# Contraction order, PSUM banks and the last gate tile of a one-core hybrid decoder layer

## The chip, the cores and the metric

The kernel runs on one core of one Trainium2 chip. A core has five engines with an instruction queue each: TensorE (PE), VectorE (DVE), ScalarE (ACT), GpSimd (POOL) and SyncE (SP); PEld in the profile is TensorE's loading of weights. The metric is the device time of one execution in microseconds; less is better.

## What is computed

One decoder layer on 512 tokens and 1024 features, all in float32. The core of the reference:

```python
x = x + 0.5 * swiglu(rmsnorm(x, ffn1_norm[i]), ffn1_wgu[i], ffn1_wdown[i])
h = rmsnorm(x, mix_norm[i])
z = h @ w_in[i]
zq, zk, zv, zc, zg = [z[..., offs[j]:offs[j + 1]] for j in range(len(SPLIT_SIZES))]
...
a = sliding_window_attention(q, k, v, sinks[i]) @ attn_proj[i]
...
u = causal_depthwise_conv(u, dw_w[i], dw_b[i])
c = jax.nn.silu(layernorm(u, conv_ln_g[i], conv_ln_b[i])) @ conv_proj[i]
ga, gb = jnp.split(zg, 2, axis=-1)
merged = jax.nn.sigmoid(ga) * a + jax.nn.sigmoid(gb) * c
x = x + merged @ w_out[i]
x = x + 0.5 * swiglu(rmsnorm(x, ffn2_norm[i]), ffn2_wgu[i], ffn2_wdown[i])
e = rmsnorm(p[i] @ ple_proj[i], ple_norm[i])
gate = jax.nn.sigmoid(rmsnorm(x, ple_gate_norm[i]) @ ple_gate_w[i])
x = x + gate * e
```

The attention has 16 query heads and 2 key/value heads of 64, a window of 128 tokens and a sink per head. `p` has 256 features.

## The kernel before

**Layout.** The activations lie with features on the 128 partitions and the 512 tokens in the free dimension: the residual is eight tiles `x[o]` of 128x512. A weight piece is 128x1024. PSUM is used as eight banks of 128x512.

**Products.** Each float32 product is made of three (`mm3`, L753): every operand is split into a rounded high half and the rest, and high by high, high by low and low by high are summed. For activations `split` makes the high half on ACT and the low half by a DVE instruction: the tiles `..._h` and `..._l`. For weights `piece` (L728) loads `raw_`, makes `whi_` on ACT and `wlo_` by a subtraction on DVE, or on DVE or POOL, whichever comes free first, for the keys in `FLEX`. For the keys in `SUMMED` (L404), the mixer's `wzc` and `wzg`, `residue` (L742) does it: ACT writes the negated rounded copy into `wlo_`, and a DMA on POOL's queue adds `raw_` to it. There are four buffers each of `raw`, `hi` and `lo` (L681).

**Stages.** FFN1, the mixer, FFN2 and the final gate follow one another on PE. The FFNs make most products in units of seven half-size products (`unit`, L972, products 1, 2, 6, 5, 7, 3, 4). `down` (L1122) adds the down products to the residual, half a tile at a time: the last unit for the first half of the outputs completes tiles 0, 1 (with product 7) and 4, 5 (product 4), that for the second half tiles 2, 3 and then 6, 7. When a tile is complete `next_norm` (L1167) splits it for the next stage (`mix_h`, `pg_h`) and adds its square to a running sum (`..._ss_acc`). The norm's factor per token is applied behind the products.

The mixer begins with keys and values: `keys_values` (L1277) calls `token_major` (L1253), whose contraction runs over the eight tiles `mix_h0` to `mix_h7` in order; two banks hold two token blocks each, and the whole contraction runs first for token blocks 0 and 1, then for 2 and 3. Queries (`wq`) go through the same function with a bank for each token block. The projections `ca`, `cb` (convolution and its gate), `ga`, `gb` (the two merge gates) are `proj` (L1180): 24 matmuls of 128x512 into a bank. `scores` (L1323), for one of two head groups `g` and one of four token blocks `t`, transposes the queries (`qTp`), then makes two groups of 12 matmuls (`jp` = 0, 1), each into two banks `sc`, each followed by the copies of ACT and the masked copies of DVE into the tiles `s` that empty them. `softmax` (L1362) makes exponentials on ACT, the denominators `den` with a reciprocal on DVE, and the normalization of `s` on POOL and ACT; `values` (L1382) transposes these (`pT`) and multiplies (`o`). The convolution is a long series of DVE instructions (`cz`) for five channel tiles, of ACT and POOL instructions for three.

`embedding` (L1485) makes the eight tiles `es` of the projected `p` during FFN2: ACT copies them out and squares them (`ple_sq`), POOL adds the squares, PE sums over partitions (`ple_cs`), and DVE multiplies each tile by its gain and by the norm's factor.

At the end, the loop from L1546 makes for each `o` the gate's product `pg` from all `pg_h` (`proj`, 24 matmuls), multiplies by the norm's factor (`wide_rstd`, whose products are `pg_mb`), takes the sigmoid on ACT, multiplies by `es`, adds to `x[o]` and stores. For the last tile these steps, but not the product, go by halves of 256 tokens.

**What sets the order.** `record` (L684) writes the program down; a planner (`plan`, L671) then orders it in the function `simulate` (L412), with costs and due times for each instruction and a list of PE groups (`nc.group`), and only then are the instructions of each engine written out (`hybrid_layer`, L1577). A group of matmuls is placed as a whole. An edit in one place can so move instructions on each engine elsewhere. `nc.flex` leaves to the planner whether DVE or POOL gets an instruction. All instructions are issued from one line, L1606, so that in the profile a group is told by its tiles.

Of the kernel before, what the change touches and what calls it, by code (L numbers as in the profile page):

```python
# [12 lines left out]
AF = mybir.ActivationFunctionType  # L13
# [3 lines left out]
P = 128  # L17
S = 512
# [665 lines left out]
def record():  # L684
    nc = Program()

    def ps_tile(name):
        return nc.tile(name, [P, S], F32, "ps")
# [70 lines left out]
    def part(w, s):  # L759
        return w[0][:, s], w[1][:, s]  # L760
# [85 lines left out]
    class SumSq:  # L846
# [3 lines left out]
        def add(self, v, on_act=False, accs=1):  # L850
# [11 lines left out]
                eng.tensor_tensor(acc, acc, to, op=ALU.add)  # L862
            self.n += 1

        def in_psum(self, v, last):

            n = self.n = self.n + 1
            to = ftile(f"{self.name}_sq{n}")
            nc.scalar.activation(to, v, AF.Square)
            if n == 1:  # L870
                self.run, self.one = ps_tile(f"{self.name}_acc"), to
            else:
                a = self.one if n == 2 else self.run
# [293 lines left out]
    def next_norm(tag, gain):  # L1167
        h, ss = [None] * KD, SumSq(f"{tag}_ss")

        def after(o):  # L1170
            h[o] = split(f"{tag}_h{o}", x[o], gain[:, o : o + 1])
            ss.in_psum(x[o], KD)

        return h, ss, after

# [4 lines left out]
    def proj(tag, key, i, h, nk=KD):  # L1180

        w = piece(key, i)
        ps = ps_tile(tag)
        with nc.group(tag):
            for k in range(nk):
                mm3(ps, part(w, slice(k * P, (k + 1) * P)), h[k], k == 0, k == nk - 1)
        return ps

    us, ys, pas = [None] * KD, [None] * KD, [None] * KD

# [59 lines left out]
        nc.gpsimd.tensor_tensor(z3[:, :, 0:16], z3[:, :, 0:16], cos, op=ALU.mult)  # L1250
        nc.gpsimd.tensor_tensor(z3[:, :, 0:16], z3[:, :, 0:16], w, op=ALU.add)

    def token_major(tag, key, i0, n_pieces, kper, n):  # L1253

        per = S // n
        banks = [ps_tile(f"{tag}b{b}") for b in range(NT // per)]
        pss = [banks[t % len(banks)][:, (t // len(banks)) * n :][:, 0:n] for t in range(NT)]
        ws = [piece(key, i0 + i) for i in range(n_pieces)]
        with nc.group(tag):
            for t0 in range(0, NT, len(banks)):  # L1260
                for i in range(n_pieces):
                    for kk in range(kper):
                        k = i * kper + kk
                        wk = part(ws[i], slice(kk * n, (kk + 1) * n))
                        for t in range(t0, t0 + len(banks)):
                            xk = part(h2[k], slice(t * P, (t + 1) * P))
                            mm3(pss[t], xk, wk, k == 0, k == KD - 1)
        return pss


# [4 lines left out]
    vf = nc.tile("vf", [P, NT, NKV, HD], F32, "a")  # L1275

    def keys_values():  # L1277
        pss = token_major("kv", "wkv", 0, 2, 4, 2 * P)
        norm2()
        k3s = []  # L1280
        for t in range(NT):
            z = nc.tile(f"zk{t}", [P, NKV, HD], F32, "a")
            p4 = pss[t].rearrange("p (b d) -> p b d", d=HD)
            r = r2k[:, t : t + 1]
            nc.scalar.activation(z, p4[:, 0:2], AF.Copy, scale=r)
            nc.scalar.activation(vf[:, t], p4[:, 2:4], AF.Copy, scale=r)
# [36 lines left out]
    def scores(g, t):  # L1323
# [12 lines left out]
        s = [nc.tile(f"s{g}_{t}_{i}", [P, 2, 2, W], F32, "a") for i in range(2)]  # L1336
        m = small(f"m{g}_{t}", 8)
        keys = slice(t0 * W, (t + 1) * W)
        for jp in range(2):
            banks = [ps_tile(f"sc{g}_{t}_{jp}{hh}") for hh in range(2)]  # L1340
            bs = [b.rearrange("p (j c k) -> p j c k", j=2, c=2) for b in banks]
            with nc.group(f"sc{g}_{t}_{jp}"):
                for j in range(2):
                    cols = slice((2 * jp + j) * P, (2 * jp + j + 1) * P)
                    for n, (a, b) in enumerate(((1, 0), (0, 0), (0, 1))):
                        for hh in range(2):
                            r = slice(hh * HD, (hh + 1) * HD)
                            nc.tensor.matmul(bs[hh][:, j, 0:nb], qT[a][r, cols], kT[b][r, keys], start=n == 0, stop=n == 2)
            for hh in range(2):
                sj = s[jp][:, :, hh]  # L1350
                if t == 0:
                    nc.vector.tensor_tensor(sj, bs[hh][:, :, 0], later, op=ALU.add)
                else:
                    nc.scalar.copy(sj, bs[hh][:, :, 1])
                    nc.vector.copy_predicated(sj, later.bitcast(I32), bs[hh][:, :, 0])
            mj = m[:, 4 * jp : 4 * jp + 4].rearrange("p (j h) -> p j h", h=2)
            nc.vector.tensor_reduce(mj, s[jp], axis=AX.X, op=ALU.max, negate=True)
# [127 lines left out]
    def embedding(i):  # L1485
# [7 lines left out]
        for j in range(4):  # L1493
# [4 lines left out]
                    c = (j * KP + k) * P  # L1498
                    mm3(ps, part(w, slice(c, c + P)), pin[k], k == 0, k == KP - 1)
            e = ftile(f"es{n}")  # L1500
            nc.scalar.copy(e, ps)
            es.append(e)
            sse.add(ps, on_act=True)
        if len(es) == KD:
            rbe = spread("ple", mean_rstd("ple", sse.accs, D))
            for o in range(KD):
                nc.vector.scalar_tensor_tensor(
                    es[o], es[o], g_ple[:, o : o + 1], rbe, op0=ALU.mult, op1=ALU.mult
                )

    steps = {
        "e": embedding,
# [31 lines left out]


    rb4 = None  # L1546
    for o in range(KD):
        ps = proj(f"pg{o}", "wgate", o, h4)
        if o == 0:
            rb4 = wide_rstd("pg", ss4.accs[0])  # L1550
        gt = ftile(f"gt{o}")
        n = S // 2 if o == KD - 1 else S
        for c in range(0, S, n):
            v = slice(c, c + n)
            nc.vector.tensor_tensor(gt[:, v], ps[:, v], rb4[:, v], op=ALU.mult)
            nc.scalar.activation(gt[:, v], gt[:, v], AF.Sigmoid)
            nc.vector.tensor_tensor(gt[:, v], gt[:, v], es[o][:, v], op=ALU.mult)
            nc.vector.tensor_tensor(x[o][:, v], x[o][:, v], gt[:, v], op=ALU.add)
# [160 lines left out]
```

## Time and profile before

| | before |
|---|---|
| runs, median (lowest to highest) | 1156.57 us (1155.35 to 1157.95) |
| profiled execution | 1154.82 us |
| its span in the trace | 1153.1 us |
| granted clock, mean | 0.999 |
| read from memory, written | 141.40 MB, 2.10 MB |

The profiled execution's span runs from its first instruction to its last; 1.7 us lie around it. In the rows of a timeline the first number is the start in us, the second the duration; x and a count joins rows of a kind, and the square bracket gives the idle time of the engine ahead of the row and what released it. PE's matmuls overlap: a row's duration is longer than the distance to the next start. The keys and values begin at 344.45 us, the embedding's sum `ple_cs` is made at 1014.36 us, and the gate begins at 1100.76 us.

### The profile page before, as it was taken

What the parts mean: (1) busy time and instruction counts of PE and PEld (TensorE: products, weight loads), DVE (VectorE), ACT (ScalarE), POOL (GpSimd) and SP (SyncE); (2) the same over time, 40 slices, a digit from 0 to 9 for tenths busy, and PEclk for the clock granted to TensorE, in tenths of its full rate; (3) what the DMA queues carried; (4) which work ended last, traced back from release to release, by engine and by line L of the source; (5) the groups of instructions that cost most, each with busy time, mean ns of one, the idle gap of its engine ahead of it and who ended that gap; (6) DMA issues with size and microseconds to landing.
All of it is one profiled execution on the core that took longest, in us unless ns stands there. A gap on an engine that the chain in (4) does not pass through costs nothing.

```text
span 1153.1 us, 19900 instructions
## 1 busy us (share of the span) xinstructions
PE 1140.8 (99%) x7484; PEld 1043.0 (90%) x7484; DVE 967.0 (84%) x1643; ACT 713.5 (62%) x1267; POOL 398.7 (35%) x481
## 2 busy tenths in 40 slices
PE   9999999999999999999999999999999999999998
PEld 7899999999998888878888888888999999999976
DVE  7799978889896799988997865579988788589995
ACT  7655446655366799999984753355654566673541
POOL 1632114222023886875786100035211132251000
PEclk9999999999999999999999999999999999999999
DMA  7456666566547472665654532335666655665421
GB/s 242 125 158 147 183 148 164 142 161 159 134 123 199 109 169 70 147 155 133 150 148 128 128 110 92 99 84 165 147 172 143 158 153 132 151 165 138 128 73 73
DMA packets 52511, 161.55 MB, mean 140 GB/s; under 512 B 6336, under 2 KB 13120, under 8 KB 52416
## 3 DMA queue, kind: packets, MB, share of 16 engines
q1 hardware_dynamic: 39312, 114.12, 30.1%
q0 software_dynamic: 12960, 46.14, 23.5%
q8 instruction: 58, 0.95, 0.3%
q14 instruction: 37, 0.30, 0.1%
q10 hardware_dynamic: 144, 0.03, 0.0%
HBM read 141.40 MB, written 2.10 MB: 124 GB/s over the span
## 4 chain that ended last, share of the span: by engine, by line
PE 94%; ACT 3%; DVE 2%; issue 0%; POOL 0%; DMA 0%; DVEq 0%; POOLq 0%; ACTq 0%
PE wgu_b L1606 17%; PE wgu_a L1606 12%; PE wd_b L1606 10%; PE wd_a L1606 8%; PE f_g L1606 5%; PE f_u L1606 5%; PE gb L1606 4%; PE ap L1606 4%; PE wo L1606 4%; PE cp L1606 4%; PE pg L1606 3%; PE cb L1606 3%; PE ga L1606 3%; PE ca L1606 3%; PE q0b L1606 2%; PE q1b L1606 2%
## 5 line engine op out<-in xcount | busy, mean ns | idle before, releaser
L1606 DVE TENSOR_TENSOR wlo_wgu<-raw_wgu,whi_wgu 128x1024 fp32r<-128x1024 f32 (+1 forms) x141 | 139.8, 1005 | 37.9 <-ACT whi_wgu L1606 37.6
L1606 ACT ACTIVATE whi_wgu<-raw_wgu 128x1024 fp32r<-128x1024 f32 (+1 forms) x141 | 115.4, 838 | 81.1 <-PE wgu_b L1606 32.7
L1606 ACT ACTIVATE whi_wd<-raw_wd 128x1024 fp32r<-128x1024 f32 (+1 forms) x60 | 59.3, 989 | 93.2 <-PE wd_b L1606 62.8
L1606 PE MATMUL wgu_b<-f_t_h,wlo_wgu 128*128 128x256 f32 x408 | 115.5, 283 | 0.0
L1606 PE MATMUL wgu_b<-f_t_l,whi_wgu 128*128 128x256 f32 x408 | 115.5, 283 | 0.0
L1606 PE MATMUL wgu_b<-f_t_h,whi_wgu 128*128 128x256 f32 x408 | 115.5, 283 | 0.0
L1606 POOL TENSOR_TENSOR y<-y,ct 128x511 f32<-128x511 f32 (+27 forms) x90 | 108.4, 1247 | 10.5 <-DVE wlo_wap L1606 5.0
L1606 DVE SCALAR_TENSOR_TENSOR cz<-u,dww,cz 128x510 f32<-128x510 f32 (+28 forms) x145 | 106.5, 735 | 3.3
L1606 POOL DMA_DIRECT2D raw_wgu<-in_wgu x34 | 29.8, 876 | 175.2 <-DMA raw_wgu<-in_wgu 53.3
L1606 PEld LDWEIGHTS wgu_b<-f_t_h,whi_wgu 128*128 128x128 f32 x408 | 78.3, 192 | 0.0
L1606 PEld LDWEIGHTS wgu_b<-f_t_h,wlo_wgu 128*128 128x128 f32 x408 | 78.3, 192 | 0.0
L1606 PEld LDWEIGHTS wgu_b<-f_t_l,whi_wgu 128*128 128x128 f32 x408 | 78.3, 192 | 0.0
L1606 PE MATMUL wgu_a<-f_nl,whi_wgu 128*128 128x256 f32 x272 | 77.0, 283 | 0.0
L1606 PE MATMUL wgu_a<-f_nh,wlo_wgu 128*128 128x256 f32 x272 | 77.0, 283 | 0.0
L1606 PE MATMUL wgu_a<-f_nh,whi_wgu 128*128 128x256 f32 x272 | 77.0, 283 | 0.0
L1606 DVE TENSOR_TENSOR wlo_wd<-raw_wd,whi_wd 128x1024 fp32r<-128x1024 f32 (+1 forms) x60 | 68.5, 1141 | 8.6 <-ACT whi_wd L1606 8.2
L1606 PE MATMUL wd_a<-f_f_h,wlo_wd 128*128 128x256 f32 x264 | 74.7, 283 | 0.0
L1606 PE MATMUL wd_a<-f_f_h,whi_wd 128*128 128x256 f32 x264 | 74.7, 283 | 0.0
L1606 PE MATMUL wd_a<-f_f_l,whi_wd 128*128 128x256 f32 x264 | 74.7, 283 | 0.0
L1606 PE MATMUL wd_b<-f_f_h,wlo_wd 128*128 128x256 f32 x264 | 74.7, 283 | 0.0
L1606 PE MATMUL wd_b<-f_f_h,whi_wd 128*128 128x256 f32 x264 | 74.7, 283 | 0.0
L1606 PE MATMUL wd_b<-f_f_l,whi_wd 128*128 128x256 f32 x264 | 74.7, 283 | 0.0
(505 smaller groups left out, 4041.2 us busy)
## 6 DMA issues: line engine op xcount, KB each, us to landing
raw_wgu<-in_wgu SPq DMA_DIRECT2D x76, 512.0 KB, 4.3
raw_wgu<-in_wgu POOLq DMA_DIRECT2D x34, 512.0 KB, 5.5
raw_wd<-in_wd SPq DMA_DIRECT2D x32, 512.0 KB, 4.5
raw_wd<-in_wd POOLq DMA_DIRECT2D x16, 512.0 KB, 5.5
raw_wzc<-in_wzc SPq DMA_DIRECT2D x16, 512.0 KB, 4.1
wlo_wzc<-raw_wzc POOLq DMA_DIRECT2D x16, 512.0 KB, 5.3
raw_wzg<-in_wzg SPq DMA_DIRECT2D x16, 512.0 KB, 4.6
wlo_wzg<-raw_wzg POOLq DMA_DIRECT2D x16, 512.0 KB, 5.8
```

Of the source, the lines that this page charges most:

```text
L1606: made[op] = getattr(engines[op.eng], op.what)(*a, **k)
```

## The change

1. `SUMMED` gets `wgate=0`: all eight gate weight pieces have their low half made by ACT and an accumulating DMA of POOL's queue.
2. `DONE = 0, 1, 4, 5, 2, 3, 6, 7`, the order in which `down` completes the residual tiles, becomes the order of the contraction for keys and values and for the first two gate tiles. These two (`proj2`) are each made as two groups of four feature tiles, which the planner may place apart.
3. `token_major` gives every token block a bank of its own, and runs through the contraction once: each feature tile is used for all four token blocks in turn. The queries had four banks already.
4. With `WHOLE` the 24 score matmuls of a block form one group into four banks, and the copies out of the banks come behind it.
5. `embedding` folds the gain into ACT's copy; what is left is a product with the norm's factor on DVE or POOL (the planner gives all eight to POOL).
6. The last gate tile is made by two groups of 24 matmuls of 128x256, each for 256 tokens and in a bank of its own (`halves`), each followed by its own steps. The other tiles go through `halves` in one piece.

`in_sbuf` isn't used, `INSB` being empty. In matmuls nothing is added but the 24 of part 6.

```diff
-SUMMED = dict(wzc=0, wzg=0)
+SUMMED = dict(wzc=0, wzg=0, wgate=0)
+WHOLE = True
+DONE = 0, 1, 4, 5, 2, 3, 6, 7
...
+    def halves(tag, key, i, h, cuts):
+        w = piece(key, i)
+        out = []
+        for c in range(cuts):
+            v = slice(c * S // cuts, (c + 1) * S // cuts)
+            out.append(ps_tile(f"{tag}_{c}"))
+            with nc.group(f"{tag}_{c}"):
+                for k in range(KD):
+                    mm3(out[c][:, v], part(w, slice(k * P, (k + 1) * P)), part(h[k], v), k == 0, k == KD - 1)
+        return out
+
+    def proj2(tag, key, os, h):
+        out = {}
+        for n in range(2):
+            for o in os:
+                if n == 0:
+                    out[o] = piece(key, o), ps_tile(f"{tag}{o}")
+                w, ps = out[o]
+                with nc.group(f"{tag}{o}_{n}"):
+                    for k in DONE[4 * n : 4 * n + 4]:
+                        mm3(ps, part(w, slice(k * P, (k + 1) * P)), h[k], k == DONE[0], k == DONE[-1])
+        return {o: ps for o, (w, ps) in out.items()}
...
-    def token_major(tag, key, i0, n_pieces, kper, n):
-        per = S // n
-        banks = [ps_tile(f"{tag}b{b}") for b in range(NT // per)]
-        pss = [banks[t % len(banks)][:, (t // len(banks)) * n :][:, 0:n] for t in range(NT)]
+    def token_major(tag, key, i0, n_pieces, kper, n, ks=range(KD)):
+        pss = [ps_tile(f"{tag}b{t}")[:, 0:n] for t in range(NT)]
         ws = [piece(key, i0 + i) for i in range(n_pieces)]
         with nc.group(tag):
-            for t0 in range(0, NT, len(banks)):
-                for i in range(n_pieces):
-                    for kk in range(kper):
-                        k = i * kper + kk
-                        wk = part(ws[i], slice(kk * n, (kk + 1) * n))
-                        for t in range(t0, t0 + len(banks)):
-                            xk = part(h2[k], slice(t * P, (t + 1) * P))
-                            mm3(pss[t], xk, wk, k == 0, k == KD - 1)
+            for k in ks:
+                i, kk = divmod(k, kper)
+                wk = part(ws[i], slice(kk * n, (kk + 1) * n))
+                for t in range(NT):
+                    xk = part(h2[k], slice(t * P, (t + 1) * P))
+                    mm3(pss[t], xk, wk, k == ks[0], k == ks[-1])
...
-        pss = token_major("kv", "wkv", 0, 2, 4, 2 * P)
+        pss = token_major("kv", "wkv", 0, 2, 4, 2 * P, DONE)
...
+        bss = []
         for jp in range(2):
...
-            with nc.group(f"sc{g}_{t}_{jp}"):
+            if not (WHOLE and jp):
+                cm = nc.group(f"sc{g}_{t}_{jp}")
+                cm.__enter__()
...
+            if not WHOLE or jp:
+                cm.__exit__(None, None, None)
+        for jp, bs in enumerate(bss):
...
-            nc.scalar.copy(e, ps)
+            nc.scalar.activation(e, ps, AF.Copy, scale=g_ple[:, n : n + 1])
...
-                nc.vector.scalar_tensor_tensor(
-                    es[o], es[o], g_ple[:, o : o + 1], rbe, op0=ALU.mult, op1=ALU.mult
-                )
+                nc.flex.tensor_tensor(es[o], es[o], rbe, op=ALU.mult)
...
+    gates = proj2("pg", "wgate", (0, 1), h4)
     for o in range(KD):
-        ps = proj(f"pg{o}", "wgate", o, h4)
+        ps = [gates[o]] if o in gates else halves(f"pg{o}", "wgate", o, h4, 2 if o == KD - 1 else 1)
```

On PE, in the keys' and values' contraction, the passage from the third to the fourth feature tile of before (`mix_h2`, `mix_h3`, the first pass over the banks `kvb0` and `kvb1`):

```order
L1606 MATMUL kvb1_4384<-whi_wkv0_4297,mix_h2_l_4346 128x256
L1606 MATMUL kvb1_4384<-whi_wkv0_4297,mix_h2_h_4331 128x256
L1606 MATMUL kvb1_4384<-wlo_wkv0_4336,mix_h2_h_4331 128x256
L1606 MATMUL kvb0_4379<-whi_wkv0_4297,mix_h3_l_4403 128x256
L1606 MATMUL kvb0_4379<-whi_wkv0_4297,mix_h3_h_4387 128x256
L1606 MATMUL kvb0_4379<-wlo_wkv0_4336,mix_h3_h_4387 128x256
```

and the passage from the second to the third in the changed kernel:

```order
L1646 MATMUL kvb3_4398<-whi_wkv0_4297,mix_h1_l_4232 128x256
L1646 MATMUL kvb3_4398<-whi_wkv0_4297,mix_h1_h_4155 128x256
L1646 MATMUL kvb3_4398<-wlo_wkv0_4337,mix_h1_h_4155 128x256
L1646 MATMUL kvb0_4379<-whi_wkv1_4341,mix_h4_l_4239 128x256
L1646 MATMUL kvb0_4379<-whi_wkv1_4341,mix_h4_h_4191 128x256
L1646 MATMUL kvb0_4379<-wlo_wkv1_4393,mix_h4_h_4191 128x256
```

The third tile used is now tile 4, from the second weight piece, after 24 matmuls for tiles 0 and 1; tile 3 comes sixth.

On PE, in the second head group's scores, the end of token block 1 and what follows (`sc1_1_10` is a bank of group 1, block 1, second pair of heads), before:

```order
L1606 MATMUL sc1_1_10_6243<-kTh_4818,qT1_1_h_6173 128x256
L1606 MATMUL sc1_1_11_6247<-kTh_4818,qT1_1_h_6173 128x256
L1606 MATMUL sc1_1_10_6243<-kTl_4835,qT1_1_h_6173 128x256
L1606 MATMUL sc1_1_11_6247<-kTl_4835,qT1_1_h_6173 128x256
L1606 MATMUL sc1_2_00_6271<-kTh_4818,qT1_2_l_6192 128x256
L1606 MATMUL sc1_2_01_6275<-kTh_4818,qT1_2_l_6192 128x256
```

and in the changed kernel:

```order
L1646 MATMUL sc1_1_10_6247<-kTh_4814,qT1_1_h_6173 128x256
L1646 MATMUL sc1_1_11_6250<-kTh_4814,qT1_1_h_6173 128x256
L1646 MATMUL sc1_1_10_6247<-kTl_4822,qT1_1_h_6173 128x256
L1646 MATMUL sc1_1_11_6250<-kTl_4822,qT1_1_h_6173 128x256
L1646 MATMUL gb7_6270<-mix_h0_h_4124,wlo_wzg15_6083 128x512
L1646 MATMUL gb7_6270<-mix_h0_h_4124,whi_wzg15_6094 128x512
```

The scores of block 2 are moved behind the 24 matmuls of the projection `gb7`, which followed them before. In the same manner the block `sc0_3` is moved behind the projections `cb4` and `cb5`, which followed it, and `ca6` now stands between `sc1_0` and `sc1_3`. On DVE the reciprocal of `den0_0` moves from behind the row of `sg2` to behind eight further rows, seven of which followed it before.

On PE, at the end of FFN2 (`wd28_1_b1` is a bank of the last down unit), before:

```order
L1606 MATMUL wd28_1_b1_12694<-f2_f20_7_h_12090,wlo_wd28_1_4_12793 128x256
L1606 MATMUL wd28_1_b1_12694<-f2_f20_7_h_12090,whi_wd28_1_4_12774 128x256
L1606 MATMUL wd28_1_b1_12694<-f2_f20_7_l_12406,whi_wd28_1_4_12774 128x256
L1606 MATMUL pg0_12873<-pg_h0_h_12646,wlo_wgate0_12817 128x512
L1606 MATMUL pg0_12873<-pg_h0_h_12646,whi_wgate0_12787 128x512
L1606 MATMUL pg0_12873<-pg_h0_l_12852,whi_wgate0_12787 128x512
```

and in the changed kernel:

```order
L1646 MATMUL pg0_12856<-pg_h5_h_12738,wlo_wgate0_12601 128x512
L1646 MATMUL pg0_12856<-pg_h5_h_12738,whi_wgate0_12802 128x512
L1646 MATMUL pg0_12856<-pg_h5_l_12852,whi_wgate0_12802 128x512
L1646 MATMUL wd28_1_b0_12667<-f2_f16_7_h_11990,wlo_wd28_1_4_12861 128x256
L1646 MATMUL wd28_1_b0_12667<-f2_f16_7_h_11990,whi_wd28_1_4_12791 128x256
L1646 MATMUL wd28_1_b0_12667<-f2_f16_7_l_12428,whi_wd28_1_4_12791 128x256
```

Before, the last down product 4 of the unit ends and the gate's first tile begins. Now the first half of `pg0` stands ahead of the 18 matmuls of product 4; behind these come the first half of `pg1`, the second halves of `pg0` and `pg1`, and then `pg_mb` and the other tiles.

On DVE at the same place, the last splits of before and the low halves of gate weights:

```order
L1606 SCALAR_TENSOR_TENSOR pg_h2_l_12887<-x2_101,g_all_68,pg_h2_h_12826 128x512
L1606 TENSOR_TENSOR pg_ss_sq8_12884<-pg_ss_acc_12725,pg_ss_sq8_12884 128x512
L1606 SCALAR_TENSOR_TENSOR pg_h3_l_12898<-x3_111,g_all_68,pg_h3_h_12871 128x512
L1606 SCALAR_TENSOR_TENSOR pg_h4_l_12902<-x4_127,g_all_68,pg_h4_h_12706 128x512
L1606 TENSOR_TENSOR pg_a_l_12907<-pg_ss_sq8_12884,pg_a_h_12900 128x512
L1606 SCALAR_TENSOR_TENSOR pg_h5_l_12911<-x5_146,g_all_68,pg_h5_h_12729 128x512
L1606 SCALAR_TENSOR_TENSOR pg_h6_l_12914<-x6_157,g_all_68,pg_h6_h_12878 128x512
L1606 SCALAR_TENSOR_TENSOR pg_h7_l_12919<-x7_168,g_all_68,pg_h7_h_12890 128x512
L1606 TENSOR_TENSOR wlo_wgate1_12924<-raw_wgate1_12672,whi_wgate1_12834 128x1024
L1606 TENSOR_TENSOR wlo_wgate2_12930<-raw_wgate2_12721,whi_wgate2_12849 128x1024
```

and in the changed kernel:

```order
L1646 SCALAR_TENSOR_TENSOR pg_h2_l_12881<-x2_101,g_all_68,pg_h2_h_12829 128x512
L1646 SCALAR_TENSOR_TENSOR pg_h3_l_12888<-x3_111,g_all_68,pg_h3_h_12869 128x512
L1646 SCALAR_TENSOR_TENSOR x6_157<-wd28_1_b0_12667,x6_157 128x256
L1646 SCALAR_TENSOR_TENSOR x7_168<-wd28_1_b1_12701,x7_168 128x256
L1646 TENSOR_TENSOR pg_ss_acc_12714<-pg_ss_acc_12714,pg_ss_sq7_12903 128x512
L1646 SCALAR_TENSOR_TENSOR pg_h6_l_12920<-x6_157,g_all_68,pg_h6_h_12910 128x512
L1646 TENSOR_TENSOR pg_ss_sq8_12916<-pg_ss_acc_12714,pg_ss_sq8_12916 128x512
L1646 SCALAR_TENSOR_TENSOR pg_h7_l_12933<-x7_168,g_all_68,pg_h7_h_12923 128x512
L1646 TENSOR_TENSOR pg_a_l_12945<-pg_ss_sq8_12916,pg_a_h_12937 128x512
L1646 TENSOR_SCALAR pg_rb_12981<-pg_mb_12975 128x512
```

The splits of tiles 4 and 5 have moved ahead of these rows, that of tile 7 is followed by the norm's factor (`pg_rb`), and no row makes a `wlo_wgate`.

More of the change, by code (lines that the diff above doesn't have):

```diff
@@ L401, in deadlines @@
         op.ls = ls
-SUMMED = dict(wzc=0, wzg=0)
+SUMMED = dict(wzc=0, wzg=0, wgate=0)
 WINDOW = 10
+WHOLE = True
+INSB = ()
+DONE = 0, 1, 4, 5, 2, 3, 6, 7
 CUT = 4
@@ L863, in add, with in_sbuf @@
             self.n += 1
+        def in_sbuf(self, v, last):
+            n = self.n = self.n + 1
+            to = ftile(f"{self.name}_sq{n}")
+            nc.scalar.activation(to, v, AF.Square)
+            if n == 1:
+                self.accs.append(to)
+            else:
+                nc.flex.tensor_tensor(self.accs[0], self.accs[0], to, op=ALU.add)
         def in_psum(self, v, last):
@@ L1171, in after @@
             h[o] = split(f"{tag}_h{o}", x[o], gain[:, o : o + 1])
-            ss.in_psum(x[o], KD)
+            (ss.in_sbuf if tag in INSB else ss.in_psum)(x[o], KD)
         return h, ss, after
@@ L1341, in scores @@
             bs = [b.rearrange("p (j c k) -> p j c k", j=2, c=2) for b in banks]
-            with nc.group(f"sc{g}_{t}_{jp}"):
+            bss.append(bs)
+            if not (WHOLE and jp):
+                cm = nc.group(f"sc{g}_{t}_{jp}")
+                cm.__enter__()
+            if 1:
                 for j in range(2):
@@ L1551, in record @@
         gt = ftile(f"gt{o}")
[L1552 to L1555, printed above, removed]
+        for i in range(len(ps)):
+            v = slice(i * S // len(ps), (i + 1) * S // len(ps))
+            nc.vector.tensor_tensor(gt[:, v], ps[i][:, v], rb4[:, v], op=ALU.mult)
             nc.scalar.activation(gt[:, v], gt[:, v], AF.Sigmoid)
```

## Prediction

> **What bounds the kernel now.** I read the page first: busy times, then the chain of work that ended last.
>
> ```profile
> PE 1140.8 (99%) x7484; PEld 1043.0 (90%) x7484; DVE 967.0 (84%) x1643; ACT 713.5 (62%) x1267; POOL 398.7 (35%) x481
> PE 94%; ACT 3%; DVE 2%; issue 0%; POOL 0%; DMA 0%; DVEq 0%; POOLq 0%; ACTq 0%
> ```
>
> TensorE is the bound: 94% of the chain. Only three things can move the time: PE's matmuls, the holes between them, and the head and tail. The waits of PE show the holes, and the table of windows how full the others are around them.
>
> ```profile
> PE sc L1606 <- DVE s L1606: 1.5, 1, 1.5
> PE kvb L1606 <- DVE mix_h_l L1606: 1.2, 1, 1.2
> PE pg L1606 <- DVE pg_h_l L1606: 1.2, 3, 0.6
> PE sc L1606 <- DVE of L1606: 0.6, 1, 0.6
> ```
>
> ```profile
> 400.00:545.00 145.00, 142.88 (x804) 118.81 (x803) 132.46 (x256) 140.81 (x312) 109.87 (x170) 1.00 0.57 135
> 985.00:1045.00 60.00, 59.56 (x453) 57.37 (x452) 43.24 (x78) 38.53 (x65) 24.53 (x25) 1.00 0.60 151
> 1100.00:1112.00 12.00, 10.73 (x47) 7.62 (x46) 12.00 (x19) 6.17 (x10) 0.00 (x0) 1.00 0.22 75
> ```
>
> The columns after the length are the busy time of PE, PEld, DVE, ACT and POOL, then the granted clock, 1.00 in all three. The holes are at the keys and values (`kvb`), the scores (`sc`) and the gate (`pg`); a fourth, at the embedding's sum, has its row below. A hole costs more than the wait on its row, since matmuls are pipelined; I take it from starts, less the usual pitch. The change touches all of them.
>
> **Keys and values.** The group's first matmul, the last ahead of the hole, the first behind it, and the group's successor:
>
> ```profile
> 344.45 0.28 PE L1606 MATMUL kvb<-whi_wkv,mix_h_l 128*128 128x256 f32 x1
> ...
> 346.49 0.28 PE L1606 MATMUL kvb<-wlo_wkv,mix_h_h 128*128 128x256 f32 x1
> 347.95 0.39 PE L1606 MATMUL kvb<-whi_wkv,mix_h_l 128*128 128x256 f32 x1 [1.18 <-DVE mix_h_l L1606]
> ...
> 357.41 0.61 PE L1606 MATMUL mix_n_cs<-ones,mix_ss_sq 128*128 128x1 f32 x5
> ```
>
> ```profile
> 341.75 2.88 DVE L1606 SCALAR_TENSOR_TENSOR mix_h_l<-x,g_all,mix_h_h 128x512 fp32r<-128x512 f32 x1
> 346.15 3.06 DVE L1606 SCALAR_TENSOR_TENSOR mix_h_l<-x,g_all,mix_h_h 128x512 fp32r<-128x512 f32 x3
> ```
>
> ```profile
> 344.78 2.55 POOL L1606 TENSOR_TENSOR wlo_wkv<-raw_wkv,whi_wkv 128x1024 fp32r<-128x1024 f32 x1
> ```
>
> 17 steps from 344.45 to 346.49 give a pitch of 0.120. The group's 96 matmuls take 12.96 us and would take 11.52: the hole costs 1.44. PE stands at feature tile 3, whose split opens the second DVE row; the last of that row's three (tiles 3, 6, 7) ends at 349.21. With four banks each tile feeds 12 matmuls, 1.44 us, and tile 3 comes sixth: at 344.45 + 5 x 1.44 = 351.65. Tiles 6 and 7 come at 353.1 and 354.5, tile 2 (split by 344.63) at 350.2. All are ready. Tight is only the second weight piece: its low half leaves POOL at 347.33, and tile 4 wants it with its third matmul, at 344.45 + 2.88 + 0.24 = 347.57. Term: **-1.44** (to -1.0 if POOL is late). The later evacuation costs nothing, since the four banks are read after `mix_n_cs` in both kernels.
>
> **Scores.**
>
> ```profile
> 445.36 0.28 PE L1606 MATMUL sc<-kTh,qT_l 64*128 64x256 f32 x1
> 446.21 0.38 PE L1606 MATMUL sc<-kTh,qT_l 64*128 64x256 f32 x1 [0.58 <-DVE of L1606]
> ...
> 501.42 0.38 PE L1606 MATMUL sc<-kTh,qT_l 64*128 64x256 f32 x1
> 503.35 0.38 PE L1606 MATMUL sc<-kTh,qT_l 64*128 64x256 f32 x1 [1.54 <-DVE s L1606]
> ```
>
> ```profile
> 502.85 1.46 DVE L1606 COPY_PREDICATED s<-masks,sc 128x256 f32<-128x256 int32 x4 [1.48 <-ACT s L1606]
> ```
>
> Less a usual step of 0.11, and with 0.10 lost in restarting, the holes are 0.84 and 1.92, together 2.76. In both a block of scores came right behind work whose banks were not yet read. In the changed order the block of 445 stands behind two whole projections, and between the two blocks at 501 stands projection `gb7`, 24 x 0.227 = 5.4 us (pitch below), so that the second would start near 507, while the first one's banks are read by 504.31 (502.85 + 1.46). Both holes go. What is late next: the reciprocal of the first block's denominators goes behind seven more DVE instructions, most of them convolution steps (`cz`). POOL's normalizations of that block wait for it, and PE's transposes `pT` for these:
>
> ```profile
> L1606 DVE SCALAR_TENSOR_TENSOR cz<-u,dww,cz 128x510 f32<-128x510 f32 (+28 forms) x145 | 106.5, 735 | 3.3
> 430.17 0.37 POOL L1606 TENSOR_SCALAR s<-s,den 128x128 f32<-128x128 f32 x1 [1.20 <-DVE den L1606]
> ...
> 434.00 0.92 POOL L1606 TENSOR_SCALAR s<-s,den 128x128 f32<-128x128 f32 x2
> ...
> 436.70 1.09 PE L1606 MATMUL pT<-ident,s 128*128 128x128 f32 x8
> ```
>
> The first normalization started at 430.17 and the last ended at 434.92, with POOL doing other things between, 1.8 us ahead of `pT`. Seven instructions at 0.735 put the start at 435.3; six normalizations at 0.37 to 0.46 then end at 437.5 to 438.1, where `pT`, now behind one more transposition, wants them at about 437: a wait of 0.5 to 1.1, less what DVE makes good. `gb7`, too, has to find a free bank. ACT, 140.81 of 145.00 us busy, leaves little to catch up with. I take 0.9 for all new waits of the stretch: **-1.86**, bounds -2.76 and +0.3 (new holes a little larger than the old ones).
>
> **Embedding.** The gain goes into an ACT copy that was made anyway: nothing. The DVE product of each tile becomes a plain one on POOL.
>
> ```profile
> 1014.36 0.83 PE L1606 MATMUL ple_cs<-ones,ple_sq 128*128 128x1 f32 x6 [0.44 <-POOL ple_sq L1606]
> ...
> L1606 POOL TENSOR_TENSOR ple_sq<-ple_sq,ple_sq x7: 1280/1290/1997, 1000.8 to 1013.0; 128x512 f32<-128x512 f32 x7
> ```
>
> `ple_cs` and the chain of squares both move about 3 us up, so its 0.6 us (wait and restart) stays: **0**, bounds -0.6 (gone) and +0.6 (doubled, as a weight load now stands among the squares). Eight products at 1.29 add 10.3 us to POOL (24.53 of 60 in this window) and take as many off DVE. Behind them in POOL's queue stand weight loads for the down product; three products, 3.9 us, precede the nearest. The row of 2.88 against 0.74 for the same instruction in other places says that DVE can be held while POOL's weight row runs. [...] DVE has 16.8 idle in the window, so that too stays under PE's work.
>
> **Gate.** PE's first matmul, the second tile's second, and the last; then DVE's last splits, and ACT's square and high half of a feature tile.
>
> ```profile
> 1100.76 0.40 PE L1606 MATMUL pg<-pg_h_h,wlo_wgate 128*128 128x512 f32 x1
> ...
> 1109.35 0.40 PE L1606 MATMUL pg<-pg_h_h,whi_wgate 128*128 128x512 f32 x1
> ...
> 1146.99 0.39 PE L1606 MATMUL pg<-pg_h_l,whi_wgate 128*128 128x512 f32 x1
> ```
>
> ```profile
> 1105.75 2.07 DVE L1606 SCALAR_TENSOR_TENSOR pg_h_l<-x,g_all,pg_h_h 128x512 fp32r<-128x512 f32 x3
> ```
>
> ```profile
> 1097.10 0.64 ACT L1606 ACTIVATE pg_ss_sq<-x 128x512 f32<-128x512 f32 x1 [1.51 <-DVE x L1606]
> 1097.64 0.71 ACT L1606 ACTIVATE pg_h_h<-x,g_all 128x512 fp32r<-128x512 f32 x1
> ```
>
> From 1109.35 to 1146.99 are 166 steps: 0.227 each. The 27 steps from 1100.76 should take 6.13 and take 8.59: the holes cost 2.46. DVE is busy 12.00 of 12.00 there, and the splits end only at 1107.82. In the change half of each of the first two tiles uses features 0, 1, 4, 5 first: 12 matmuls, 2.72 us, stand ahead of the last 18 down matmuls (2.16 us at 0.120), and 2.72 behind them. On the old clock these begin at 1098.60 and 1101.3, the down products end at 1103.5, and the second halves begin at 1106.2, wanting tiles 2 and 3 at once and tile 7 from 1108.3, its split with the third matmul, 1108.7. After the last down matmul, tile 7 needs DVE's last addition (0.4, 1103.9), ACT's two squares and two high halves (2.7, 1106.6) and the split (0.7, as a third of 2.07): 1107.3, with 1.4 to spare. Tile 3's last product ends 9 matmuls ahead of the gate's first, at 1097.5, so tiles 2 and 3 have over 8 us for the same steps. The low halves of the last two down weights now stand close ahead of their products; I keep 0.2 for them. Term **-2.26**, bounds -2.46 and 0.
>
> The weights' low halves leave DVE for a second ACT copy and an accumulating DMA of POOL's queue, as the mixer's have it:
>
> ```profile
> 500.84 1.05 ACT L1606 ACTIVATE wlo_wzc<-raw_wzc 128x1024 fp32r<-128x1024 f32 x1
> 431.03 0.87 POOL L1606 DMA_DIRECT2D wlo_wzc<-raw_wzc  x1 [0.49 <-ACT wlo_wzc L1606]
> wlo_wzg<-raw_wzg POOLq DMA_DIRECT2D x16, 512.0 KB, 5.8
> 1093.45 0.85 ACT L1606 ACTIVATE whi_wd<-raw_wd 128x768 fp32r<-128x768 f32 x1 [2.10 <-issue]
> ```
>
> 1.05 + 0.87 + 5.8 = 7.7 us. Piece 1 is the nearest: its copy stands just ahead of the 1093.45 row, so it lands near 1101.2, for a use at 1103.5. Hidden, with 2.3 to spare. The eight copies cost ACT 8.4 us, of which it has 5.8 idle in the 1100 to 1112 row alone.
>
> **Last tile and tail.** 24 matmuls at 0.227 (5.45) become 48 at 0.120 (5.76): **+0.31**. The end:
>
> ```profile
> 1147.42 0.75 DVE L1606 TENSOR_TENSOR gt<-pg,pg_rb 128x256 f32<-128x256 f32 x2 [2.63 <-PE pg L1606]
> 1149.00 0.75 DVE L1606 TENSOR_TENSOR x<-x,gt 128x256 f32<-128x256 f32 x2
> ```
>
> Now one half is left behind the last matmul: four steps of about 0.41 with 0.03 between them end at 1149.17, not 1149.75: **-0.6**.
>
> **Sum.** -1.44 - 1.86 + 0 - 2.26 + 0.31 - 0.6 = -5.85 us. The profiled execution took 1154.82 us (span 1153.1, 1.7 around it): 1148.97. The median of the three runs is 1156.57, which makes **1150.7**. A measurement of this kernel can tell about 0.2%, 2.3 us, from no change.
>
> **The rivals.**
> *Nothing new in the scores' favour (14%).* New waits eat the 2.76, since ACT is 97% busy in that stretch, and a tight low half costs 1 us at the gate: about -3 us, 1153.6. For it speaks that the order changes all through 400 to 545 and ACT has 4 us to spare; against it that PE, under the same load, has just two holes there.
> *Little moves (8%).* The waits are only renamed: the gate's splits still late, the scores' holes elsewhere. Kv and the tail remain, -1.44 + 0.31 - 0.6: about 1154.8. Against it: the 1.4 us to spare at the gate.
> *Slower (5%).* The gate's low halves arrive late. If only one piece is under way at a time, each tile takes 7.7 us instead of 5.45, from tile 2 on: 6 x 2.3 = 13.8, less the 5.85 gained: +8, 1164.5. It decides once a landing takes more than 5.8 + 2.3. Against it: DMA's share is 0.22 in the gate, and 0.57 where 5.8 was measured. [...]
>
> **How the numbers follow.** My forecast has 73%. The best sum, all gaps gone, is -1.44 - 2.76 - 0.6 - 2.46 - 0.3 = -7.6, 1149.0, and a median itself scatters by about 1; the first rival ends at 1153.6 and the second at 1154.8. The range is 1148.0 to 1154.6. Faster by over 0.2%: the forecast and two thirds of the first rival, 0.82; within 0.2%: the rest of it and the second, 0.13; slower 0.05.
>
> **What would show it.** In the new profile: no `kvb` wait on `mix_h_l`; none of `sc` on `s`; `pT` on POOL's `s` under 1 us; the `pg` waits on `pg_h_l` gone, none on `wlo_wgate`; 48 matmuls `pg` of 128x256; `ple_cs` waiting about as long. A span over 1150, or a wait of PE over 1.5 us anywhere, would make it wrong.

## The result and the profile after

| | before | changed |
|---|---|---|
| runs, median (lowest to highest) | 1156.99 us (1155.35 to 1157.95) | 1150.92 us (1150.64 to 1151.36) |
| profiled execution, its span | 1154.82 us, 1153.1 us | 1150.64 us, 1148.7 us |

Four runs of each on the same chip give a ratio of 0.9949, 95% interval 0.9932 to 0.9967. The forecast was 1150.7. The medians lie 6.07 us apart, the two traces only 4.39 (spans 1153.12 and 1148.73); most of the rest lies in what one trace of the kernel before doesn't show (the two clusters, below).

The changed kernel's busy times, its chain, and its waits of PE in full:

```profile
PE 1141.1 (99%) x7508; PEld 1044.4 (91%) x7508; DVE 957.7 (83%) x1628; ACT 719.7 (63%) x1273; POOL 422.2 (37%) x496
...
PE 90%; ACT 4%; DVE 3%; POOL 1%; issue 1%; DMA 0%; POOLq 0%; ACTq 0%; DVEq 0%
```

```profile
PE warm L1646 <- DVE ones L1646: 1.1, 1, 1.1
PE q1b L1646 <- DVE of L1646: 0.4, 1, 0.4
PE ple_cs L1646 <- POOL ple_sq L1646: 0.4, 1, 0.4
PE f_g L1646 <- DVE wlo_wgu L1646: 0.3, 1, 0.3
PE ga L1646 <- DVE s L1646: 0.3, 1, 0.3
PE gb L1646 <- DVE sga L1646: 0.2, 1, 0.2
```

The waits at `kvb`, at `sc` and at `pg` are gone; behind the first matmuls (`warm`) none is longer than 0.4 us. Three small ones are new: `q1b`, `ga` and `gb`. The stretches, with busy time of PE, PEld, DVE, ACT, POOL, then clock and DMA share (moved by the shift that has built up):

```profile
398.30:543.30 145.00, 144.03 (x805) 118.34 (x804) 132.49 (x260) 138.38 (x309) 108.40 (x168) 1.00 0.55 132
983.00:1043.00 60.00, 59.56 (x450) 57.03 (x450) 45.18 (x77) 39.27 (x66) 30.86 (x29) 1.00 0.57 147
1097.20:1109.00 11.80, 11.80 (x63) 10.12 (x62) 7.71 (x13) 9.46 (x13) 2.05 (x3) 1.00 1.00 261
```

At the gate DVE has fallen from 12.00 of 12.00 to 7.71 of 11.80 and PE has no hole. In the scores' stretch PE's idle time has fallen only from 2.12 to 0.97, with ACT at 138.38.

The places of the prediction on PE: first matmul of keys and values and their successor, the first of the convolution norm's product `ln_mb`, that of the first `wd24` down product, which follows the embedding, the first of the gate, that of its third tile, and the last; then the steps behind it.

```profile
344.46 0.28 PE L1646 MATMUL kvb<-whi_wkv,mix_h_l 128*128 128x256 f32 x1
...
355.98 0.50 PE L1646 MATMUL mix_n_cs<-ones,mix_ss_sq 128*128 128x1 f32 x4
...
631.85 0.39 PE L1646 MATMUL ln_mb<-ln_s_h,mean_r 128*128 128x512 f32 x1
...
1028.76 0.28 PE L1646 MATMUL wd_b<-f_f,wlo_wd 128*128 128x256 f32 x1
...
1097.21 0.40 PE L1646 MATMUL pg<-pg_h_h,wlo_wgate 128*128 128x512 f32 x1
...
1110.77 0.40 PE L1646 MATMUL pg<-pg_h_h,wlo_wgate 128*128 128x512 f32 x1
...
1143.64 0.28 PE L1646 MATMUL pg<-pg_h_l,whi_wgate 128*128 128x256 f32 x1
```

```profile
1143.95 0.42 DVE L1646 TENSOR_TENSOR gt<-pg,pg_rb 128x256 f32<-128x256 f32 x1 [1.01 <-PE pg L1646]
...
1145.32 0.42 DVE L1646 TENSOR_TENSOR x<-x,gt 128x256 f32<-128x256 f32 x1
1145.77 0.33 SPq L1646 DMA_DIRECT2D out_T<-x  x1
```

The three of these landmarks that the rows ahead of the prediction don't have, before:

```profile
633.55 0.39 PE L1606 MATMUL ln_mb<-ln_s_h,mean_r 128*128 128x512 f32 x1
...
1030.20 0.28 PE L1606 MATMUL wd_b<-f_f,wlo_wd 128*128 128x256 f32 x1
...
1114.58 0.39 PE L1606 MATMUL pg<-pg_h_h,wlo_wgate 128*128 128x512 f32 x1
```

From landmark to landmark, the traces' 4.39 us divide so:

| stretch | before | changed | difference | term of the prediction |
|---|---|---|---|---|
| first `kvb` to `mix_n_cs` | 12.96 | 11.52 | -1.44 | -1.44 |
| to `ln_mb` (scores) | 276.14 | 275.87 | -0.27 | -1.86 |
| to `wd24` (embedding) | 396.65 | 396.91 | +0.26 | 0 |
| to third gate tile | 84.38 | 82.01 | -2.37 | -2.26 |
| to the end | 38.54 | 37.96 | -0.58 | +0.31 - 0.6 |

### The profile page after: what moved, and what is told of

Its sections match the earlier page's. It is cut to its first block, busy times and chain, and to the rows that moved or that the text cites. A ratio compares the mean times of both kernels' runs of the same rounds, so it can differ in the third digit from the quotient of the medians.

```text
span 1148.7 us, 19972 instructions
## 1 busy us (share of the span) xinstructions
PE 1141.1 (99%) x7508; PEld 1044.4 (91%) x7508; DVE 957.7 (83%) x1628; ACT 719.7 (63%) x1273; POOL 422.2 (37%) x496
## 4 chain that ended last, share of the span: by engine, by line
PE 90%; ACT 4%; DVE 3%; POOL 1%; issue 1%; DMA 0%; POOLq 0%; ACTq 0%; DVEq 0%
PE wgu_b L1646 17%; PE wgu_a L1646 13%; PE wd_b L1646 11%; PE wd_a L1646 8%; PE f_g L1646 5%; PE f_u L1646 5%; PE pg L1646 4%; PE ap L1646 4%; PE wo L1646 4%; PE cp L1646 4%; PE ga L1646 3%; PE gb L1646 3%; PE cb L1646 2%; PE ca L1646 2%; PE q0b L1646 2%; ACT s L1646 1%
## 5 line engine op out<-in xcount | busy, mean ns | idle before, releaser
L1646 POOL TENSOR_TENSOR y<-y,ct 128x511 f32<-128x511 f32 (+28 forms) x90 | 112.6, 1309 | 9.4 <-DVE wlo_wap L1646 5.0
L1646 DVE SCALAR_TENSOR_TENSOR cz<-u,dww,cz 128x509 f32<-128x509 f32 (+27 forms) x145 | 106.1, 735 | 2.8
L1646 DVE TENSOR_TENSOR wlo_wd<-raw_wd,whi_wd 128x1024 fp32r<-128x1024 f32 (+1 forms) x60 | 72.2, 1203 | 9.4 <-ACT whi_wd L1646 8.6
```

The lines of the kernel that those rows point to most:

```text
L1646: made[op] = getattr(engines[op.eng], op.what)(*a, **k)
```

## The experiments

Each expectation was on record before its run. As the start of the first `kvb` scatters between 344.45 and 345.33 us from one execution to the next, whatever the kernel (see the end), the table also gives the time from there to the end of the span: 808.67 us before, 804.27 in the changed kernel.

| kernel | median (range), us | span | from `kvb` on, against changed |
|---|---|---|---|
| `kv_order_plain` | 1151.66 (1151.52 to 1151.79) | 1149.6 | +0.59 |
| `kv_two_banks` | 1152.88 (1152.63 to 1152.98) | 1150.8 | +1.83 |
| `gate_one_group` | 1152.72 (1152.32 to 1153.02) | 1150.7 | +1.59 |
| `gate_lo_on_dve` | 1152.56 (1152.25 to 1152.73) | 1150.5 | +1.67 |
| `es_on_dve` | 1152.37 (1152.07 to 1152.55) | 1150.2 | +1.20 |
| `last_tile_whole` | 1152.09 (1151.43 to 1152.62) | 1149.9 | +0.49 |
| `scores_two_groups` | 1152.70 (1151.81 to 1153.63) | 1150.0 | +0.55 |
| `fewer_taps` | 1149.43 (1149.07 to 1149.82) | 1148.1 | -1.45 |
| `before_one_group` | 1154.05 (1153.78 to 1155.35) | 1152.1 | +3.28 |
| `one_group_g1` | 1154.22 (1153.83 to 1154.93) | 1153.2 | +3.62 |

**Keys and values: banks or order.** The first kernel keeps the four banks and drops the order, the second the reverse.

```diff
-        pss = token_major("kv", "wkv", 0, 2, 4, 2 * P, DONE)
+        pss = token_major("kv", "wkv", 0, 2, 4, 2 * P)
```

> The changed kernel, but the keys' and values' contraction goes over the feature tiles 0 to 7 in plain order, still with a bank for each token block. My theory: the banks alone take the hole away, since each tile then feeds 1.44 us of PE, so that tile 3 is wanted 4.3 us after the group's first matmul, about 0.9 us after its split is done; no wait at kvb over 0.2 us, span within 0.5 us of the changed kernel's 1148.7. Rival: the order of completion is what does it; then kvb waits 0.5 to 1.4 us on mix_h_l and the span is longer by as much.

No wait at `kvb` in the list, as my theory had it. The stretch from `kvb` to `mix_n_cs` takes 11.68 us, 0.16 more, lost in its first four steps. Most of the 0.59 us is elsewhere: from `ln_mb` to `wd24` 0.38 are lost, with a wait of 0.4 us for ACT's `es`.

```diff
-        pss = [ps_tile(f"{tag}b{t}")[:, 0:n] for t in range(NT)]
+        per = S // n
+        banks = [ps_tile(f"{tag}b{b}") for b in range(NT // per)]
+        pss = [banks[t % len(banks)][:, (t // len(banks)) * n :][:, 0:n] for t in range(NT)]
...
+            for t0 in range(0, NT, len(banks)):
                 for k in ks:
...
-                for t in range(NT):
+                    for t in range(t0, t0 + len(banks)):
```

> The changed kernel, but keys and values in two banks and two passes again, in the order 0, 1, 4, 5, 2, 3, 6, 7. My theory: the order alone doesn't help, because tile 4 is then wanted 1.44 us after the group's first matmul and the low half of the second weight piece comes only 2.9 us after it; kvb waits 1.2 to 1.8 us, on wlo_wkv instead of mix_h_l, and the span is 1.0 to 1.8 us longer than the changed kernel's 1148.7. Rival: the order alone does it; no wait at kvb over 0.3 us and the same span.

```profile
346.27 0.28 PE L1649 MATMUL kvb<-whi_wkv,mix_h_h 128*128 128x256 f32 x1
347.65 0.39 PE L1649 MATMUL kvb<-wlo_wkv,mix_h_h 128*128 128x256 f32 x1 [1.10 <-POOL wlo_wkv L1649]
```

With the order alone the hole stays, 1.26 us instead of 1.34, and only its releaser changes: from the split of tile 3 to the second weight piece. The stretch takes 12.88 us, against 12.96 before; the rest of the 1.83 us is mostly the same 0.38 at the embedding. The banks made the gain; the order, alone or behind them, gave next to nothing for keys and values.

**The gate: which relief counts.** Three parts of the change take work off DVE there or give it time: the two groups each of the first two tiles, the weights' low halves, and the embedding's products. Each was undone by itself.

```diff
-    gates = proj2("pg", "wgate", (0, 1), h4)
+    gates = {}
```

> The changed kernel, but the first two gate tiles are made like the others, each in one group over tiles 0 to 7 behind the last down products; the low halves of the gate weights stay off DVE. My theory: most of the gate's gain comes from the order and the two groups; with DVE relieved of the weights alone, pg still waits for the splits, 0.8 to 2 us in all, and the span is 0.8 to 2 us longer than 1148.7. Rival: DVE's relief alone does it; pg waits under 0.4 us in all.

```profile
1097.55 0.28 PE L1646 MATMUL wd_b<-f_f_l,whi_wd 128*128 128x256 f32 x1
1099.12 0.39 PE L1646 MATMUL wd_b<-f_f_h,wlo_wd 128*128 128x256 f32 x1 [1.29 <-DVE wlo_wd L1646]
```

The size was as expected, the place wasn't: the wait is a step earlier, at the last down product, whose low half comes late; the first gate tile had lain in front of it and hidden that.

```diff
-SUMMED = dict(wzc=0, wzg=0, wgate=0)
+SUMMED = dict(wzc=0, wzg=0)
```

> The changed kernel, but the low halves of the gate weights are subtracted on DVE again (eight of 1.22 us); the first two gate tiles keep their two groups each. My theory: the 1.4 us to spare at the last split go to the two pieces that come ahead of it on DVE; pg waits 0.3 to 1.2 us in all, and the span is 0.3 to 1.2 us longer than 1148.7. Rival: the two groups alone are enough; no wait at pg over 0.2 us, same span.

```profile
1101.88 0.39 PE L1646 MATMUL pg<-pg_h_h,whi_wgate 128*128 128x512 f32 x1
1103.59 0.50 PE L1646 MATMUL pg<-pg_h_l,whi_wgate 128*128 128x512 f32 x1 [1.33 <-DVE pg_h_l L1646]
```

The wait is at the place expected, and above my upper end of 1.2 us: 1.33 on the row, 1.67 from `kvb` on.

```diff
-                nc.flex.tensor_tensor(es[o], es[o], rbe, op=ALU.mult)
+                nc.vector.tensor_tensor(es[o], es[o], rbe, op=ALU.mult)
```

> The changed kernel, but the eight products of the embedding with its norm's factor are made on DVE (about 0.7 us each) instead of POOL. My theory: DVE has room for them, as its relief at the gate comes from the weights; no new wait at pg over 0.3 us, span within 0.4 us of 1148.7. Rival: they land among the splits, and pg waits 0.5 to 1.5 us.

```profile
1093.04 0.28 PE L1646 MATMUL wd_a<-f_f_l,whi_wd 128*128 128x256 f32 x1
1094.31 0.39 PE L1646 MATMUL wd_a<-f_f_h,wlo_wd 128*128 128x256 f32 x1 [0.98 <-DVE wlo_wd L1646]
```

My theory falls: DVE had no room for them. The rival named the wrong place (`pg`) but the right size: the low half of a down weight comes 1 us late. So the gate's 2.37 us need all three: with any one undone, 1.2 to 1.7 us are lost again.

**The last tile.**

```diff
-        ps = [gates[o]] if o in gates else halves(f"pg{o}", "wgate", o, h4, 2 if o == KD - 1 else 1)
+        ps = [gates[o]] if o in gates else halves(f"pg{o}", "wgate", o, h4, 1) * (2 if o == KD - 1 else 1)
```

> The changed kernel, but the product of the last gate tile is one group of 24 matmuls of 128x512 as before; the steps behind it still go by halves of 256 tokens. My theory: the last matmul starts 0.3 to 0.5 us earlier, and the tail behind it is 0.9 to 1.0 us longer, so that the span is 0.4 to 0.7 us longer than 1148.7. Rival: the halves gain nothing, since their 48 matmuls cost as much as the shorter tail brings; span within 0.2 us.

From `kvb` on the last matmul starts 0.39 us earlier and the tail behind it is 0.88 longer (5.97 against 5.09): 0.49 in sum, as expected. The medians lie 1.17 apart; of the rest the traces show nothing.

**The scores.** The first kernel goes back to two groups. The second leaves out the later half of the convolution's taps for the three channel tiles of ACT and POOL, so that it computes another result, with no matmul less: it only makes the stretch's load lighter.

```diff
-WHOLE = True
+WHOLE = False
```

> The changed kernel, but the scores of a block are made in two groups of 12 matmuls with two banks each again, each emptied before the next is needed. The trace of the changed kernel has lost both holes of the scores (0.95 and 1.92 us) and yet the whole stretch from the norm's sum to the convolution's norm is only 0.27 us shorter than before. My theory: that stretch is set by how much ACT and DVE have to do, so that the way the scores are grouped only decides where PE waits; the stretch is within 0.6 us of the changed kernel's 275.9, with other holes. Rival: the one group of 24 gains what the holes cost and something else lost it; without it the stretch is 1.5 to 3 us longer. If the scores are also what makes the times of the kernel before fall into two clusters (1155.0 to 1155.3 and 1156.7 to 1158.0), the times of this kernel do too.

```profile
PE sc L1646 <- DVE s L1646: 1.5, 1, 1.5
PE warm L1646 <- DVE ones L1646: 1.1, 1, 1.1
PE ple_cs L1646 <- POOL ple_sq L1646: 0.7, 1, 0.7
PE sc L1646 <- DVE of L1646: 0.6, 1, 0.6
```

Both old holes are back and the small new waits gone; the stretch is 276.16 us long, against 275.87. In one profiled execution, then, the one group of 24 gains next to nothing. But three of the six runs lay at 1151.81 to 1152.03 and three at 1153.37 to 1153.63. The kernel before has two such clusters. Of its 54 runs beside the experiments, 25 have spans of 1153.1 to 1153.8 us and a mean granted clock of 0.999 or 1.000, and 29 have spans of 1154.7 to 1155.4 and a clock of 0.997 or 0.998, with none between.

```diff
-        for d in [*range(2, TAPS), 1] if ext else range(1, TAPS):
+        for d in [*range(2, TAPS), 1] if ext else range(1, TAPS // 2):
```

> The changed kernel without the later half of the convolution's taps (15 to 30) for the three channel tiles that ACT and POOL compute: 48 ACT instructions of about 0.7 us and 48 additions of POOL of about 1.3 us are left out, no matmul. My theory (ACT and DVE, busy 138 and 132 of 145 us, set the small waits of the scores' stretch): PE's new waits there (q1b on of, gb on sga, ga on s, pT on s and their restarts, about 2.5 us in all) fall under 1 us and the span is 1 to 2.5 us shorter than 1148.7. Rival: the waits come from the chain of single steps between a score and its use, whatever else ACT has to do; span within 0.6 us of 1148.7.

```profile
398.30:543.30 145.00, 144.70 (x807) 119.34 (x807) 130.65 (x260) 132.47 (x298) 99.96 (x158) 1.00 0.57 133
```

The waits at `q1b`, `ga` and `gb` are gone; PE idles 0.30 us of the window instead of 0.97, and from `kvb` on 1.45 us are gained. At `ga` and `gb` PE's order around the wait is unchanged, so that the load of ACT, DVE and POOL makes these waits, as my theory had it; which of the three the runs don't tell. At `q1b` it isn't shown, because four matmuls `o` have moved from behind the scores ahead of it to before them.

**The two clusters.** Two kernels were run once more, unchanged, for a second trace, the one group of 24 was made alone on the kernel before, and it was kept for the second head group alone in the changed kernel.

> The kernel before, unchanged, for a second profiled execution. If it falls into the upper cluster (1156.7 or more), its trace shows where the 1.7 us are: my theory, in one longer wait of PE at the scores; rival, spread over the whole span or ahead of the first matmul. If it falls into the lower one it says only that the first trace repeats within 0.5 us in every stretch.

It took 1157.34 us: upper cluster. Its waits of PE are those of the first trace, but for one of 0.3 us that is missing. These are the windows behind the second hole of the scores (502.65 to 504.17 here), with the granted clock as the third column from the end:

```profile
504.00:506.00 2.00, 1.83 (x24) 1.66 (x25) 2.00 (x8) 1.98 (x4) 2.00 (x3) 0.92 0.97 213
506.00:508.00 2.00, 2.00 (x5) 1.61 (x6) 2.00 (x5) 1.99 (x7) 1.67 (x3) 0.50 0.57 107
508.00:510.00 2.00, 2.00 (x8) 1.53 (x8) 2.00 (x5) 2.00 (x4) 1.11 (x2) 0.73 0.10 10
510.00:512.00 2.00, 2.00 (x10) 1.66 (x9) 0.92 (x4) 1.39 (x3) 2.00 (x2) 1.00 0.76 250
```

In the first trace, of the lower cluster, the clock stays at 1.00 behind the same hole:

```profile
506.00:508.00 2.00, 2.00 (x10) 1.68 (x9) 2.00 (x5) 2.00 (x6) 1.67 (x2) 1.00 0.32 59
```

In the upper cluster PE is busy behind the hole, but it does half as much: the clock is at 0.50 for about 3.4 us, and matmuls of 128x512 start 0.43 us apart instead of 0.23:

```profile
506.43 0.63 PE L1606 MATMUL gb<-mix_h_h,whi_wzg 128*128 128x512 f32 x1
506.85 0.63 PE L1606 MATMUL gb<-mix_h_l,whi_wzg 128*128 128x512 f32 x1
507.28 0.63 PE L1606 MATMUL gb<-mix_h_h,wlo_wzg 128*128 128x512 f32 x1
```

The stretch from `q1b` to `ln_mb` takes 173.46 us here, 171.88 in the lower cluster's trace: 1.58 more. No wait of PE shows this.

> The changed kernel with the scores in two groups again, unchanged, for a second profiled execution. If it falls into the upper cluster (1153.4 or more), its trace shows where the 1.7 us are: my theory, in one longer wait of PE at the scores; rival, spread over the whole span or ahead of the first matmul. If it falls into the lower one it says only that its first trace repeats.

1153.09 us, and the same: the clock at 0.50 behind the second hole, a stretch longer by 1.56 us (173.46 against 171.90).

> The kernel before with one edit: the 24 score matmuls of a block are one group in four banks, as in the changed kernel. My theory: the grouping is what the two clusters of times hang on (three runs of the changed kernel with two groups lay at 1151.8 to 1152.0 and three at 1153.4 to 1153.6), so this kernel has one cluster, and the trace, which has so far caught only lower-cluster runs of such kernels, gains less than 0.8 us in the stretch from the norm's sum to the convolution's norm (276.1 before). All runs within 1 us of each other, median 0.5 to 2 us under that of the kernel before. Rival: the clusters belong to another part; the times still fall into two, 1.5 us or more apart.

One cluster: ten of 11 runs within 1.0 us, the eleventh 0.6 above them, and the spans are all 1152.1 to 1152.9. The median is 2.33 us under that of the kernel before beside it, 1156.38, more than I expected; but that run has a span of the lower cluster, 1153.5, and the medians of the spans are only 1.4 apart. The trace gains 1.12 from `kvb` on, 0.24 of it in the scores' stretch and 0.65 in the next, where the wait of `ple_cs` is gone. The grouping is what the clusters hang on.

```diff
-            if not (WHOLE and jp):
+            if not (WHOLE and g and jp):
...
-            if not WHOLE or jp:
+            if not (WHOLE and g) or jp:
```

> The changed kernel, with the scores of the first head group in two groups of 12 again and those of the second in one of 24: of the two old holes only the first, 0.85 us at the scores sc0_3, comes back. In two profiled executions of the upper cluster the granted clock falls to 0.50 for about 3.4 us some 1.5 us behind the second hole (1.9 us), and nowhere else. My theory: only that hole is long enough for this, so the times form one cluster, all within 1 us, with the hole at sc on of near 0.6 us in the waits, and the median within 0.8 us of the changed kernel's 1150.9. Rival: the shorter hole brings the clock down in some executions too; two clusters 1.3 us or more apart.

One cluster again, 11 runs from 1153.83 to 1154.93, with the first hole (0.59 us at `sc` on `of`) in the trace: in none of these runs did it bring the clock down (a mean of 0.999 or 1.000 in all). The median is 2.5 us above my upper end; the trace shows other waits in the planner's new order (`pT` 1.0, `gb` 0.9, `ga` 0.8).

## Why the prediction was right, and where not

The time came out within 0.3 us of the forecast, but in part by luck. Trace against trace the kernel gained 4.39 us and not the 5.85 of the sum: the profiled execution was forecast at 1148.97 and took 1150.64. The median gained 6.07 because three of the four runs of before lay, by their times, in its upper cluster. By the shares of the clusters (29 of 54), I estimate from the runs that the mean gain is 4.39 + 0.54 x 1.6 = 5.3 us.

**Keys and values** (-1.44): right in size and mechanism. Of its two parts the banks alone do it.

**Scores** (-1.86): wrongly sized twice, and the two errors nearly cancel in the median. First, "I take 0.9 for all new waits" was too little: the two holes of 2.76 are gone, and the stretch is only 0.27 shorter, so the new waits cost about 2.5. That is close to my first rival, in which new waits eat the 2.76. These are the two longest:

```profile
461.47 0.40 PE L1646 MATMUL q1b<-wlo_wq,mix_h_h 128*128 128x512 f32 x1
462.28 0.50 PE L1646 MATMUL q1b<-whi_wq,mix_h_l 128*128 128x512 f32 x1 [0.41 <-DVE of L1646]
...
509.24 0.50 PE L1646 MATMUL ga<-mix_h_h,wlo_wzg 128*128 128x512 f32 x1 [0.27 <-DVE s L1646]
```

`q1b` costs 0.7 with its restart and `ga` about 0.8 with the transposes ahead of it; I had seen neither. `pT` costs 0.3, less than I said, and `gb7`, which I named without a price, 0.3. The remaining 0.4 or so I can't place. `fewer_taps` wins 1.45 of the 2.5 back, so that the load of the stretch makes a good part of them. Second, the hole of 1.92 us was priced at its own length, because the windows that I read gave a clock of 1.00. That was the lower cluster. In the upper cluster, 29 of the 54 runs of before, the hole also cost 1.6 us of halved clock (1.58 in the trace of `before_again`), and where the second head group's scores were made in one group of 24, no run here shows the second cluster.

**Embedding** (0): the place itself cost +0.26. But "take as many off DVE" was given no value, and `es_on_dve` shows that it is worth 1.2 us: DVE makes these products from 1063 to 1081 us there, and the wait comes at 1094, where DVE prepares the last down weights.

**Gate** (-2.26): -2.37. The splits came in time, and the two close low halves show no wait. The late weights of the slower rival didn't come about: a piece landed 4.5 to 7.7 us after its issue, below the 8.1 from which I had it decide, although the DMA share is 1.00 there now and not the 0.22 that I argued from.

**Last tile and tail** (-0.29): -0.58. The matmuls cost 0.34, about what was said (from the third tile to the first step behind the last matmul), and the four steps gained 0.54. Not foreseen were 0.38 us from the last step to the end of the span. Part of it stands in the store's rows, that of the changed kernel above (1145.77) and this of before:

```profile
1149.45 0.81 SPq L1606 DMA_DIRECT2D out_T<-x  x2
```

The last store's issue ends 0.51 us behind the last addition before and 0.36 now, as it no longer stands behind its other half's; where the other 0.23 come from is open.

## What to carry to other kernels

Look for the engine behind the wait before counting it: at the gate three separate parts were each needed, and with any one missing PE waited 1.0 to 1.3 us at another row for the same engine. At the keys and values a bank for each output, so that an operand tile feeds twice the work, took the hole of 1.34 us away, and the order of the operands did not (1.26). And price a hole of PE by several executions: one trace shows its length (1.92 us at the scores), the scatter of the run times may show the clock (1.6 us more in 29 of 54 runs).

## What was not expected of the hardware

A pause of PE of 1.5 us, between score matmuls, was followed by a granted clock of 0.50 for about 3.4 us in some executions and not in others of the same kernel. In `one_group_g1`, which has of the two old holes only the shorter, a pause of 0.6 us, none of the 11 runs shows this: the mean clock is 0.999 or 1.000 in all.

In `before_again` the pause lasts from 502.65 to 504.17 us, and the clock falls at about 505.7, some 1.5 us behind it, which I estimate from the 0.92 of the window from 504 to 506. In `two_groups_again`, with a wait of the same 1.5 us at `sc`, it falls at about 503.6: it is 0.95 from 500 to 504 and 0.50 from 504 to 506. In the first trace of before the pause is as long (501.80 to 503.35), and so is the wait in that of `scores_two_groups` (1.5), but there the clock stays up, with a mean of 0.999 and 1.000. So the length of the pause alone doesn't decide it, and what does, no run here shows. In the ten other traces no wait of PE is longer than 1.33 us (`gate_lo_on_dve`), and the mean clock is 0.999 or 1.000; what a pause between 1.33 and 1.5 us does, no run here shows either.

The scatter of the first `kvb` is most likely the clock again, at the start: in `before_again`, where it is at 345.28, the early matmuls of 128x512 start 0.43 us apart until 7.25, as they do behind the hole at a clock of 0.50; in the first trace, where it is at 344.45, they are 0.23 apart from 6.01 on.

```profile
6.40 0.63 PE L1606 MATMUL f_g<-h_l,whi_wgu 128*128 128x512 f32 x1
6.83 0.63 PE L1606 MATMUL f_u<-h_h,whi_wgu 128*128 128x512 f32 x1
7.25 0.44 PE L1606 MATMUL f_u<-h_h,wlo_wgu 128*128 128x512 f32 x1
7.53 0.39 PE L1606 MATMUL f_u<-h_l,whi_wgu 128*128 128x512 f32 x1
```
